# Twelve split halves, a Newton root on VectorE and modulation rows along the free axis, in a three-layer transformer kernel

## The chip, the cores and the metric

The kernel runs on one core of a Trainium2 chip as one program. The metric is device time in microseconds: the median of 3 runs of the kernel before is 1167.11 us (1166.7 to 1167.43). The engines are TensorE (PE, with weight loads shown apart as PEld), VectorE (DVE), ScalarE (ACT), GpSimd (POOL) and SyncE (SP), which here only issues DMAs.

## The reference, in short

256 tokens of width 1024 in f32 go through two layers of one kind and one of another.

```python
for l in range(2):
    h = rms_norm(x, g_pre_mix[l]);  z = h @ w_in[l]          # q, k, v, cb, cc, cx, ga, gb
    y_attn = band_attention(rope(q), rope(k), v, sink) @ w_attn_proj[l]
    y_conv = (cb * short_conv(cc * cx, conv_w[l])) @ w_conv_proj[l]
    mix = (sigmoid(ga) * y_attn + sigmoid(gb) * y_conv) @ w_out[l]
    x = x + rms_norm(mix, g_post_mix[l])
    h = rms_norm(x, g_pre_ffn[l])
    x = x + rms_norm((silu(h @ w_gate[l]) * (h @ w_up[l])) @ w_down[l], g_post_ffn[l])
mod = silu(c) @ w_cond + b_cond                              # 6 rows of 1024: shift, scale, gate, twice
h = rms_norm(x, g_mix_pre) * (1 + scale_m) + shift_m
mix = concat(stick_breaking(q, k, v), pooling(u)) @ w_out;   x = x + gate_m * rms_norm(mix, g_mix_post)
h = rms_norm(x, g_ffn_pre) * (1 + scale_f) + shift_f
x = x + gate_f * rms_norm((silu(h @ w_gate) * (h @ w_up)) @ w_down, g_ffn_post)
```

`rms_norm(x, g)` is `x * rsqrt(mean(x*x) + 1e-6) * g`, along the row of a token.

## The kernel before, in words

**Split products.** Every f32 product is made of two or three products of a rounded type. A value is cast to its high part H on ACT (`nc.scalar.copy`, L277 for weights, L208 for activations) and DVE subtracts to get the low part L (L279, L209). Then H x H, H x L and L x H are added up in PSUM.

**The weight stream.** The host packs all weights in the order of use into chunks of 128 x 2048 f32 (1 MB, `ORDER`). `emit_raw` (L250) issues one DMA for a chunk on SP's queue into one of `NRAW` = 4 buffers (the first four chunks in two halves each). `emit_half` (L266) splits half a chunk into an H and an L tile of 128 x 1024; there are `NSPLIT` = 9 of each. `get` (L283) hands out the next chunk, and emits loads up to 5 chunks and splits up to 3 chunks ahead; its `cap` bounds the splits, at L506 and L587 to `NSPLIT` halves counted from the oldest chunk still held. `behind` (L262) places a split in its engine's order after a named instruction: ACT's casts after the last square of the latest norm, DVE's subtractions after its scaling.

**Order.** The program hands its instructions to a framework, which fixes each engine's order at build time from the program's order, the dependencies and its own estimates; on the chip each engine keeps to that order. The program itself interleaves independent work by generators with due times on a clock of PE work (`spawn`, `tick`, `pe`): the transposes of a norm (`Norm.tr`) come `TR_DELAY` = 6.0 us of PE work after the post norm before them. `hp()` raises the priority of the norms' operations.

**Norms.** The tokens lie in two tiles of 128, t = 0 and 1, in `xt`. A stage's output products fill two PSUM halves for t = 0, then two for t = 1 (`row_out`, L486: 3 chunks x 2 halves x 6 products for each tile). After each half, `Post.half` squares and sums it on ACT (`sumsq`, L354, and a small add, L355) and multiplies it by the gain row on DVE (L422). `Post.fin` takes the root (`rstd`, L358: a power of -0.5 on POOL, L360) and adds the scaled half to x on DVE (L429). Then `Norm.vec` does the same for the next norm: squares on ACT, x times the gain row on DVE (L378), the root on POOL, the scaling on DVE (L384; L386 with a shift row; L382 for the very first norm, whose gain is applied after the transposes, L401). PE transposes the result (L395), ACT and DVE split it (`Pair.put`, L208 and L209), and the next stage's products can begin. In the FFN these are `pgA` and `puA` for t = 0 (24 products each), then for t = 1.

**Start.** 13 products on ones run first, then the first norm, then `q_first` (L700), the q projection in an order of its own.

**Conditioning.** The six modulation rows are computed beside layers 0 and 1. `cond_chunk` (L516) takes 256 rows of `w_cond` at a time, adds w times silu(c), a column scalar, into an accumulator of 128 x 1024 (L527, twice a chunk, 24 chunks), then GpSimd sums it over the partitions (L530), and a row goes to DRAM (`modd`). `get_rows` (L965) fetches the gain and modulation rows for the next norm by DMA, broadcast over the partitions, where the last three down chunks' outputs begin; it is called from `mkpost`.

**Buffers.** Large activation tiles (4 KB a partition) come from a pool of `NS4` = 17.

Of the kernel before, what the change touches and what calls it, by code (L numbers as in the profile page):

```python
# [10 lines left out]
F32 = mybir.dt.float32  # L11
F32R = mybir.dt.float32r
AF = mybir.ActivationFunctionType
ALU = mybir.AluOpType
# [20 lines left out]
WARM = 13  # L35
NRAW = 4
NSPLIT = 9
LOOK = 3
LOOK_RAW = 5
NS4 = 17  # L40
NS2 = 7
# [75 lines left out]
def pack_weights(inp):  # L117
# [10 lines left out]
    for i, k in enumerate(ORDER):  # L128
# [31 lines left out]
def tile_model(ctx: ExitStack, tc: tile.TileContext, x_in, wpack, sink, convw, gains, c_in, g0t_in,  # L160
# [101 lines left out]
    def behind(e):  # L262

        return tc.issue_after(state["behind"][e].ins) if state["behind"] and state["spl"] + e else nullcontext()

    def emit_half():  # L266
        i, hf = divmod(state["spl"], 2)
        while state["raw"] <= i:
            emit_raw()
        if ORDER[i][0] == "cond":  # L270
            HL[i] = raws[i]
        else:
            H = wp.tile([P, CH // 2], F32R, tag="H", name=f"H{i}_{hf}", bufs=NSPLIT)
            L = wp.tile([P, CH // 2], F32R, tag="L", name=f"L{i}_{hf}", bufs=NSPLIT)
            rv = raws[i][:, hf * (CH // 2):(hf + 1) * (CH // 2)]
            with behind(0):
                nc.scalar.copy(H, rv)  # L277
            with behind(1):
                nc.vector.tensor_sub(L, rv, H.bitcast(F32))  # L279
            HL.setdefault(i, []).append((H, L))  # L280
        state["spl"] += 1

    def get(key, cap=None):  # L283
# [3 lines left out]
        n = len(ORDER)  # L287
        while state["raw"] < min(i + LOOK_RAW, n):
            emit_raw()
# [16 lines left out]

    warm = cst.tile([P, 512], mybir.dt.bfloat16, tag="warm", name="warm")
    nc.vector.memset(warm, 1.0)
# [7 lines left out]
    for i in range(WARM):  # L316
        mm(pw, warm[:, 0:P], warm, i == 0, i == WARM - 1)
    emit_raw()
    emit_raw()
    nc.sync.dma_start(xt[1], x_in[P:2 * P, :])  # L320
    nhalf = cst.tile([P, 1], F32, tag="nhalf", name="nhalf")
    nc.vector.memset(nhalf, -0.5)
    eps = cst.tile([P, 1], F32, tag="eps", name="eps")
# [3 lines left out]
    modd = dr.tile([6, D], F32, tag="modd", name="modd")  # L327
    silu_c = cst.tile([P, KT], F32, tag="silu_c", name="silu_c")
# [4 lines left out]
    csb = cst.tile([P, KT], F32, tag="csb", name="csb")  # L333
    pscale = cst.tile([P, 4], F32, tag="pscale", name="pscale")

    def late_consts():
# [5 lines left out]
        nc.sync.dma_start(cw, convw)  # L342
        nc.sync.dma_start(csb, c_in)
        nc.sync.dma_start(pscale, pool_scale)
# [6 lines left out]
    def sumsq(src, c, ssq, name):  # L351

        junk = s2(f"jk_{name}{c}")
        nc.scalar.activation(junk, src, AF.Square, scale=D ** -0.5, accum_out=ssq[:, c:c + 1])  # L354
        return nc.scalar.activation(ssq[:, c:c + 1], ssq[:, c:c + 1], AF.Identity,  # L355
                                    bias=eps if c == 0 else ssq[:, 0:1])

    def rstd(ssq, name):  # L358
        rs = small("rs_" + name, 1)
        nc.gpsimd.tensor_tensor(rs, ssq[:, 1:2], nhalf, ALU.pow)  # L360
        return rs

    class Norm:
# [6 lines left out]
        def vec(self):  # L370
            t, name = self.t, self.name
            with hp():
                ssq = small("sx_" + name, 2)
                xg = s4("xg_" + name)
                for c in range(2):
                    self.sq = sumsq(xt[t][:, HC[c]], c, ssq, "x" + name)
                    if self.cols is None:
                        nc.vector.tensor_mul(xg[:, HC[c]], xt[t][:, HC[c]], self.G[:, HC[c]])  # L378
                rs = rstd(ssq, "x" + name)
                for c in range(2):  # L380
                    if self.cols is not None:
                        self.sc = nc.vector.tensor_scalar(xg[:, HC[c]], xt[t][:, HC[c]], rs[:, 0:1], None, ALU.mult)  # L382
                    elif self.S is None:
                        self.sc = nc.vector.tensor_scalar(xg[:, HC[c]], xg[:, HC[c]], rs[:, 0:1], None, ALU.mult)  # L384
                    else:
# [123 lines left out]

    cacc = [None]  # L510

    def cond_due():
# [3 lines left out]
    def cond_chunk(key):  # L516
        w = get(key).rearrange("p (h k c) -> p k h c", k=2, h=2)
        r, j = key[1], key[2]
        if j == 0:
            a = s4(f"cacc{r}")  # L520
            nc.vector.memset(a, 0.0)
            nc.scalar.dma_start(a[0:1, :], b_cond[r:r + 1, :])
            cacc[0] = a
        a = cacc[0]
        for k in range(2):
            a3 = a.rearrange("p (h c) -> p h c", h=2)
            nc.vector.scalar_tensor_tensor(a3, w[:, k], silu_c[:, 2 * j + k:2 * j + k + 1], a3, ALU.mult, ALU.add)  # L527
        if j == 3:
            mrow = s4(f"mrow{r}")
            nc.gpsimd.partition_all_reduce(mrow, a, P, bass_isa.ReduceOp.add)  # L530
            nc.scalar.dma_start(modd[r:r + 1, :], mrow[0:1, :])

    def ffn(l, xp, norms, make_post, after):
        order = [k for k in ORDER if k[0] in ("g", "u", "d") and k[1] == l]
# [27 lines left out]
        for key in order:  # L562
# [137 lines left out]
    def q_first(q, xp):  # L700
# [28 lines left out]
        spawn(norms[1].gen, 1.0)  # L729
        w[1, 0] = get(("q", 0, 1, 0), 8)  # L730
        run(0, 1, (0,))
# [9 lines left out]
    def mixer1(l, xp, norms):  # L741
# [198 lines left out]


    xp = Pair("x0")
    norms = [Norm(t, None, None, xp, f"n0{t}", g0t) for t in range(2)]
# [3 lines left out]
    for l in range(DEPTH):  # L947
# [43 lines left out]

        ffn(l, xp, norms, mkpost, after2)
        xp, norms = nxp, nn
# [121 lines left out]
```

## Time and profile before

| | |
|---|---|
| median of 3 runs | 1167.11 us (1166.7 to 1167.43) |
| profiled execution: own time, span | 1168.2 us, 1166.2 us |
| mean granted clock of TensorE | 0.996 |
| PE busy | 1147.2 us, 98% |
| DVE, ACT, POOL busy | 829.4, 694.7, 55.3 us |
| read from HBM | 232.76 MB, 201 GB/s over the span |

In rows of instructions, the first two numbers are the start in the span and the duration, in us; "x4" is a count of merged instructions; what stands in brackets at the end is how long the engine was idle before, and what ended that. In rows of waits, the numbers are the total, the count and the longest, in us. In rows of stretches, each engine has its busy time and count, and then come PE's granted clock, the busy share of the DMA engines and GB/s. A matmul's end is modelled, so neighbouring matmuls overlap: from one start to the next counts, not the duration.

### The profile page before, as it was taken

The page shows a single profiled execution, that of the slowest core. Times are in us where ns is not written, and L with a number is a line of the kernel's source. Part 1 is how long each engine was busy: PE and PEld are TensorE (multiplying, and loading weights), DVE is VectorE, ACT ScalarE, POOL GpSimd, SP SyncE. Part 2 cuts the span into 40 slices and gives each one's busy share as a digit, 9 for nine tenths or more (in the row PEclk, how much of TensorE's full clock was granted, in tenths as well). Part 3 has the DMA queues.
Part 4 walks back from the last instruction along what each step waited for, and adds up shares of the span by engine and source line. Part 5 has one row for each costly group of instructions (what it writes and reads, how often), then busy time and mean ns, then how long its engine had stood idle before and what let it go on. Part 6 is the DMA issues. An engine that isn't in the chain of part 4 may idle for free.

```text
span 1166.2 us, 15511 instructions
## 1 busy us (share of the span) xinstructions
PE 1147.2 (98%) x5909; PEld 957.3 (82%) x5909; DVE 829.4 (71%) x1149; ACT 694.7 (60%) x1219; POOL 55.3 (5%) x34
## 2 busy tenths in 40 slices
PE   8999999999999999999999999999999999999997
PEld 5888888878888887888888878888877777888886
DVE  6788835869788858787757678887958438766652
ACT  6777856556555447688856456545456546655451
POOL 0000000001102000000020002020200001000000
PEclk8999999999999999999999999999999999999999
DMA  9633335657576664534457647675766245654620
GB/s 330 257 144 113 141 144 210 228 212 266 204 290 221 249 250 181 217 114 139 145 190 290 226 146 268 246 271 212 286 230 248 104 162 181 253 184 177 211 79 36
DMA packets 36386, 234.83 MB, mean 201 GB/s; under 512 B 4812, under 2 KB 5324, under 8 KB 9816
## 3 DMA queue, kind: packets, MB, share of 16 engines
q1 hardware_dynamic: 33552, 224.82, 52.9%
q10 hardware_dynamic: 2760, 9.03, 2.4%
q8 instruction: 46, 0.75, 0.3%
q14 instruction: 28, 0.23, 0.1%
HBM read 232.76 MB, written 1.07 MB: 201 GB/s over the span
## 4 chain that ended last, share of the span: by engine, by line
PE 89%; ACT 4%; DVE 3%; DMA 1%; issue 1%; POOL 1%; SPq 0%; DVEq 0%; POOLq 0%; ACTq 0%
PE pu L244 14%; PE dn L244 14%; PE pg L244 13%; PE pq L244 4%; PE pcx L244 4%; PE pcp L244 4%; PE wo L244 4%; PE pap L244 4%; PE pga L244 4%; PE pgb L244 4%; PE pcb L244 3%; PE pgA L244 2%; PE puA L244 2%; PE pcc L244 2%; PE pkv L244 2%; PE po L244 2%
## 5 line engine op out<-in xcount | busy, mean ns | idle before, releaser
L279 DVE TENSOR_TENSOR L<-raw,H 128x1024 fp32r<-128x1024 f32 x374 | 470.8, 1271 | 182.5 <-ACT H L277 171.3
L277 ACT CAST H<-raw 128x1024 fp32r<-128x1024 f32 x374 | 390.0, 1050 | 182.9 <-PE pg L244 35.5
L244 PE MATMUL dn<-H,fHL 128*128 128x512 f32 x432 | 116.1, 390 | 0.0
L244 PE MATMUL pu<-xf,H 128*128 128x512 f32 x432 | 108.2, 392 | 0.0
L244 PE MATMUL pg<-xf,H 128*128 128x512 f32 x432 | 107.8, 391 | 0.0
L244 PEld LDWEIGHTS dn<-H,fHL 128*128 128x128 f32 x432 | 79.8, 188 | 15.6
L244 PEld LDWEIGHTS pg<-xf,H 128*128 128x128 f32 x432 | 79.2, 188 | 15.2
L244 PEld LDWEIGHTS pu<-xf,H 128*128 128x128 f32 x432 | 77.7, 189 | 13.9
L244 PE MATMUL dn<-L,fHL 128*128 128x512 f32 x216 | 66.6, 389 | 0.0
L244 PEld LDWEIGHTS pg<-xf,L 128*128 128x128 f32 x432 | 58.9, 190 | 4.2
L244 PEld LDWEIGHTS pu<-xf,L 128*128 128x128 f32 x432 | 58.9, 190 | 4.2
L527 DVE SCALAR_TENSOR_TENSOR cacc<-raw,silu_c,cacc 128x1024 f32<-128x1024 f32 x48 | 61.3, 1277 | 0.2
L244 PE MATMUL pu<-xf,L 128*128 128x256 f32 x432 | 60.2, 282 | 0.0
L244 PE MATMUL pg<-xf,L 128*128 128x256 f32 x432 | 60.2, 282 | 0.0
L530 POOL PARTITION_ALL_REDUCE mrow<-cacc x6 | 38.9, 6489 | 346.6 <-PE po L244 138.3
L244 PE MATMUL wo<-H,m 128*128 128x512 f32 x192 | 52.4, 395 | 0.0
L573 ACT CAST fHL<-f 128x512 fp32r<-128x512 f32 x27 | 16.7, 619 | 56.1 <-DVE f L571 56.1
L244 PEld LDWEIGHTS dn<-L,fHL 128*128 128x128 f32 x216 | 40.6, 188 | 8.6
L244 PEld LDWEIGHTS wo<-H,m 128*128 128x128 f32 x192 | 35.5, 188 | 7.4 <-DVE m L209 0.2
L567 ACT ACTIVATE s<-s 128x512 f32<-128x512 f32 x27 | 17.1, 632 | 33.0 <-DVE s L454 33.0
L244 PE MATMUL pcp<-H,y 128*128 128x512 f32 x128 | 35.4, 396 | 0.0
L244 PE MATMUL pap<-H,o 128*128 128x512 f32 x128 | 35.2, 394 | 0.0
(283 smaller groups left out, 1980.4 us busy)
## 6 DMA issues: line engine op xcount, KB each, us to landing
raw<-in_wpack_dram SPq DMA_DIRECT2D x207, 1024.0 KB, 5.0
raw<-in_wpack_dram SPq DMA_DIRECT2D x8, 512.0 KB, 7.0
gpm<-in_gains_dram ACTq DMA_DIRECT2D x3, 512.0 KB, 6.2
gpf<-in_gains_dram ACTq DMA_DIRECT2D x3, 512.0 KB, 9.2
gqf<-in_gains_dram ACTq DMA_DIRECT2D x2, 512.0 KB
out_dram<-x SPq DMA_DIRECT2D x4, 256.0 KB, 2.0
pmat<-in_pmat_dram SPq DMA_DIRECT2D x2, 384.0 KB, 5.9
x<-in_x_dram SPq DMA_DIRECT2D x2, 256.0 KB, 2.9
```

The source lines that it names most:

```text
L244: nc.tensor.matmul(o, a, b, start=start, stop=stop, **kw)
L277: nc.scalar.copy(H, rv)
L279: nc.vector.tensor_sub(L, rv, H.bitcast(F32))
L527: nc.vector.scalar_tensor_tensor(a3, w[:, k], silu_c[:, 2 * j + k:2 * j + k + 1], a3, ALU.mult, ALU.add)
L530: nc.gpsimd.partition_all_reduce(mrow, a, P, bass_isa.ReduceOp.add)
L567: last = nc.scalar.activation(s, s, AF.Silu)
L573: nc.scalar.copy(fHL[:, 0], fv)
```

## The change

- Raw weights come in halves of a chunk: 8 buffers of 128 x 1024, one DMA each. There are 12 H and 12 L tiles instead of 9. The large activation tiles fall from 17 to 15; the build reserves less scratch, and some constants move into pools.
- The very first split cast is placed behind the first norm's squares on ACT.
- `sumsq` keeps one small add (mean + eps of the first half) and drops the second; `rstd` now adds, guesses the root by integer operations and takes three Newton steps, nine operations on DVE, in place of the power on POOL. In norms without a shift row the gain is multiplied in the scaling itself (scalar_tensor_tensor) and not before it.
- Conditioning weights are packed so that a partition holds output columns and the input runs along the free axis. silu(c) is a row broadcast to all partitions (in a large activation tile), DVE multiplies and sums along the row in one operation per half chunk, and the reduction on GpSimd goes. c and b_cond are now fetched on ACT's queue in layer 0's gates.
- `get_rows` is also called at the down chunk five before the end (`early`), two chunks before the tail.

```diff
-NRAW = 4
-NSPLIT = 9
+NRAW = 8
+NSPLIT = 12
-NS4 = 17
+NS4 = 15
...
         elif n == "cond":
-            put(i, inp["w_cond_2"][0], 256 * k[2], 2, 1024 * k[1], 1024)
+            w = inp["w_cond_2"][0][:, 1024 * k[1]:1024 * (k[1] + 1)].reshape(D, P, KT)
+            out[i].reshape(P, 2, D)[...] = w[:, :, 2 * k[2]:2 * k[2] + 2].transpose(1, 2, 0)
...
     def emit_raw():
-        i = state["raw"]
-        t = wp.tile([P, CH], F32, tag="raw", name=f"raw{i}", bufs=NRAW)
-        n = 2 if i < 4 else 1
-        for h in range(n):
-            hs = slice(h * CH // n, (h + 1) * CH // n)
-            if i == 0 and h == 1:
-                nc.vector.tensor_copy(t[:, hs.start:hs.start + 1], xt[0][:, 0:1])
-            state["dma"] = nc.sync.dma_start(t[:, hs], wpack[i][:, hs])
-        raws[i] = t
+        i, hf = divmod(state["raw"], 2)
+        t = wp.tile([P, CH // 2], F32, tag="raw", name=f"raw{i}_{hf}", bufs=NRAW)
+        if state["raw"] == 1:
+            nc.vector.tensor_copy(t[:, 0:1], xt[0][:, 0:1])
+        state["dma"] = nc.sync.dma_start(t, wpack[i][:, hf * (CH // 2):(hf + 1) * (CH // 2)])
+        raws[2 * i + hf] = t
         state["raw"] += 1
 
     def behind(e):
-        return tc.issue_after(state["behind"][e].ins) if state["behind"] and state["spl"] + e else nullcontext()
+        if state["spl"] + e == 0:
+            return tc.issue_after(norms[0].sq.ins)
+        return tc.issue_after(state["behind"][e].ins) if state["behind"] else nullcontext()
...
     def sumsq(src, c, ssq, name):
         junk = s2(f"jk_{name}{c}")
-        nc.scalar.activation(junk, src, AF.Square, scale=D ** -0.5, accum_out=ssq[:, c:c + 1])
-        return nc.scalar.activation(ssq[:, c:c + 1], ssq[:, c:c + 1], AF.Identity,
-                                    bias=eps if c == 0 else ssq[:, 0:1])
+        i = nc.scalar.activation(junk, src, AF.Square, scale=D ** -0.5, accum_out=ssq[:, c:c + 1])
+        if c == 0:
+            i = nc.scalar.activation(ssq[:, 0:1], ssq[:, 0:1], AF.Identity, bias=eps)
+        return i
 
     def rstd(ssq, name):
-        rs = small("rs_" + name, 1)
-        nc.gpsimd.tensor_tensor(rs, ssq[:, 1:2], nhalf, ALU.pow)
-        return rs
+        w = small("nw_" + name, 3)
+        m, y, t = (w[:, i:i + 1] for i in range(3))
+        nc.vector.tensor_scalar(m, ssq[:, 1:2], ssq[:, 0:1], -0.5, ALU.add, ALU.mult)
+        nc.vector.tensor_scalar(y.bitcast(I32), m.bitcast(I32), 0x7FFFFFFF, 1, ALU.bitwise_and, ALU.logical_shift_right)
+        nc.vector.tensor_scalar(y.bitcast(I32), y.bitcast(I32), -1, 0x5F3759DF - (1 << 22), ALU.mult, ALU.add)
+        for _ in range(3):
+            nc.vector.scalar_tensor_tensor(t, y, m, y, ALU.mult, ALU.mult)
+            nc.vector.scalar_tensor_tensor(y, t, 1.5, y, ALU.add, ALU.mult)
+        return y
...
-                    if self.cols is None:
+                    if self.S is not None:
                         nc.vector.tensor_mul(xg[:, HC[c]], xt[t][:, HC[c]], self.G[:, HC[c]])
...
                     elif self.S is None:
-                        self.sc = nc.vector.tensor_scalar(xg[:, HC[c]], xg[:, HC[c]], rs[:, 0:1], None, ALU.mult)
+                        self.sc = nc.vector.scalar_tensor_tensor(xg[:, HC[c]], xt[t][:, HC[c]], rs[:, 0:1],
+                                                                 self.G[:, HC[c]], ALU.mult, ALU.mult)
...
     def cond_chunk(key):
-        w = get(key).rearrange("p (h k c) -> p k h c", k=2, h=2)
+        w = get(key)
         r, j = key[1], key[2]
-        if j == 0:
-            a = s4(f"cacc{r}")
-            nc.vector.memset(a, 0.0)
-            nc.scalar.dma_start(a[0:1, :], b_cond[r:r + 1, :])
-            cacc[0] = a
-        a = cacc[0]
-        for k in range(2):
-            a3 = a.rearrange("p (h c) -> p h c", h=2)
-            nc.vector.scalar_tensor_tensor(a3, w[:, k], silu_c[:, 2 * j + k:2 * j + k + 1], a3, ALU.mult, ALU.add)
+        for u in range(2):
+            nc.vector.scalar_tensor_tensor(w[u], w[u], 1.0, silu_c, ALU.mult, ALU.mult,
+                                           accum_out=mcol[:, r, 2 * j + u:2 * j + u + 1])
         if j == 3:
-            mrow = s4(f"mrow{r}")
-            nc.gpsimd.partition_all_reduce(mrow, a, P, bass_isa.ReduceOp.add)
-            nc.scalar.dma_start(modd[r:r + 1, :], mrow[0:1, :])
+            nc.vector.tensor_add(mcol[:, r], mcol[:, r], bcol[:, r])
+            nc.scalar.dma_start(modd[r].rearrange("(p j) -> p j", p=P), mcol[:, r])
 
-    def ffn(l, xp, norms, make_post, after):
+    def ffn(l, xp, norms, make_post, after, early=lambda: None):
...
+                if j == NDOWN - TAIL - 2:
+                    early()
...
-        w[1, 0] = get(("q", 0, 1, 0), 8)
+        w[1, 0] = get(("q", 0, 1, 0), 6)
...
             if l == 0 and c == 0:
+                csb = s4("csb")
+                nc.scalar.dma_start(csb, c_in[0].partition_broadcast(P))
+                nc.scalar.dma_start(bcol, b_cond)
                 nc.scalar.activation(silu_c, csb, AF.Sigmoid)
                 nc.vector.tensor_mul(silu_c, silu_c, csb)
...
+    silu_c = s4("silu_c")
...
-        ffn(l, xp, norms, mkpost, after2)
+        ffn(l, xp, norms, mkpost, after2, get_rows)
...
-    nc = _bacc.Bacc("TRN2", target_bir_lowering=False, num_devices=1)
+    nc = _bacc.Bacc("TRN2", target_bir_lowering=False, num_devices=1, dynamic_dma_scratch_size=1024)
```

More of the change, by code (lines that the diff above doesn't have):

```diff
@@ L12 @@
 F32R = mybir.dt.float32r
+I32 = mybir.dt.int32
 AF = mybir.ActivationFunctionType
@@ L250, in emit_raw @@
     def emit_raw():
[L251 to L259 removed]
+        i, hf = divmod(state["raw"], 2)
[4 more added lines that the diff above has]
+        raws[2 * i + hf] = t
         state["raw"] += 1
     def behind(e):
[L264 removed]
+        if state["spl"] + e == 0:
+            return tc.issue_after(norms[0].sq.ins)
+        return tc.issue_after(state["behind"][e].ins) if state["behind"] else nullcontext()
     def emit_half():
[L267 to L268 removed]
+        n = state["spl"]
+        i, hf = divmod(n, 2)
+        while state["raw"] <= n:
             emit_raw()
+        r = raws.pop(n)
         if ORDER[i][0] == "cond":
[L271 removed]
+            HL.setdefault(i, []).append(r)
         else:
@@ L287, in get @@
         n = len(ORDER)
-        while state["raw"] < min(i + LOOK_RAW, n):
+        while state["raw"] < 2 * min(i + LOOK_RAW, n):
             emit_raw()
@@ L305, in row @@
         return g
-    warm = cst.tile([P, 512], mybir.dt.bfloat16, tag="warm", name="warm")
+    warm = s2("warm", (P, 512), mybir.dt.bfloat16)
     nc.vector.memset(warm, 1.0)
@@ L317, in tile_model @@
         mm(pw, warm[:, 0:P], warm, i == 0, i == WARM - 1)
-    emit_raw()
-    emit_raw()
+    for i in range(4):
+        emit_raw()
     nc.sync.dma_start(xt[1], x_in[P:2 * P, :])
-    nhalf = cst.tile([P, 1], F32, tag="nhalf", name="nhalf")
-    nc.vector.memset(nhalf, -0.5)
     eps = cst.tile([P, 1], F32, tag="eps", name="eps")
@@ L327, in tile_model @@
     modd = dr.tile([6, D], F32, tag="modd", name="modd")
-    silu_c = cst.tile([P, KT], F32, tag="silu_c", name="silu_c")
+    mcol = cst.tile([P, 6, KT], F32, tag="mcol", name="mcol")
+    bcol = cst.tile([P, 6, KT], F32, tag="bcol", name="bcol")
     amask = cst.tile([P, 2, P], F32, tag="amask", name="amask")
@@ L332, in tile_model @@
     cw = cst.tile([P, DEPTH, KT, 3], F32, tag="cw", name="cw")
-    csb = cst.tile([P, KT], F32, tag="csb", name="csb")
     pscale = cst.tile([P, 4], F32, tag="pscale", name="pscale")
@@ L508, in mix_out @@
         row_out(ch, accs, lead > 0, make_post, after)
-    cacc = [None]
     def cond_due():
@@ L1095 @@
         ("gains", np.stack(g)),
-        ("c", inp["c_2"].reshape(KT, P).T),
+        ("c", inp["c_2"].reshape(1, D)),
         ("g0t", inp["g_pre_mix"][0].reshape(KT, P).T),
-        ("b_cond", inp["b_cond_2"].reshape(6, D)),
+        ("b_cond", inp["b_cond_2"].reshape(6, P, KT).transpose(1, 0, 2)),
         ("w_pool", inp["w_pool_2"][0].transpose(1, 0, 2)),
```

6 lines of the change are left out of this document (2 added, 4 removed).

## The prediction

> **What bounds the kernel now.** I read the page's busy shares first, then TensorE's own waits.
>
> ```profile
> span 1166.2 us, 15511 instructions
> PE 1147.2 (98%) x5909; PEld 957.3 (82%) x5909; DVE 829.4 (71%) x1149; ACT 694.7 (60%) x1219; POOL 55.3 (5%) x34
> ```
>
> ```profile
> PE pt_n L395 <- DVE xg_n L382: 2.3, 1, 2.3
> PE pt_nm L395 <- DVE xg_nm L386: 2.0, 2, 1.8
> PE pgA L244 <- DVE xf L209: 2.0, 3, 1.0
> ...
> PE pq L244 <- DVE xm L209: 0.9, 1, 0.9
> ```
>
> TensorE (PE) is busy for all but 1166.2 - 1147.2 = 19.0 us, and the change takes no product away, so everything it can win lies in those 19 us and in the time in which PE runs slowly. The waits lie at the norms: the first one (pt_n), the handovers where a norm feeds the next stage (pgA, pq), and the norm that needs modulation rows (pt_nm). The start in order of time, and then three stretches of it (busy times of PE, PEld, DVE, ACT, POOL, then PE's granted clock):
>
> ```profile
> 5.00 0.28 ACT L355 ACTIVATE sx_n<-sx_n,eps 128x1 f32<-128x1 f32 x1
> ...
> 6.74 1.04 ACT L277 CAST H<-raw 128x1024 fp32r<-128x1024 f32 x1 [1.46 <-DMA raw<-in_wpack_dram]
> ...
> 8.06 0.57 POOL L360 TENSOR_TENSOR rs_xn<-sx_n,nhalf 128x1 f32<-128x1 f32 x1 [7.63 <-ACT sx_n L355]
> 8.66 0.88 DVE L382 TENSOR_SCALAR xg_n<-x,rs_xn 128x512 f32<-128x512 f32 x2 [4.51 <-POOL rs_xn L360]
> ...
> 9.21 1.38 PE L395 MATMUL pt_n<-ident,xg_n 128*128 128x128 f32 x8 [2.33 <-DVE xg_n L382]
> ...
> 11.08 6.68 PE L244 MATMUL pq<-H,x 128*128 128x512 f32 x16 [0.49 <-ACT x L208]
> ```
>
> ```profile
> 6.88:9.20 2.32, 0.00 (x0) 0.00 (x0) 0.54 (x2) 1.10 (x2) 0.57 (x1) 1.00 0.85 279
> 9.87:16.69 6.82, 6.33 (x17) 4.30 (x16) 6.75 (x10) 5.66 (x9) 0.00 (x0) 0.50 1.04 389
> 16.69:25.30 8.61, 8.61 (x43) 7.12 (x42) 7.54 (x11) 5.68 (x13) 0.57 (x1) 1.00 0.97 371
> ```
>
> The sums of squares are ready by 5.28 but for one small add on ScalarE (ACT), and that add stands behind a split cast that waits for its weights until 6.74. Then PE stands still for 2.32 us, its clock is halved for 6.82 us, and DVE is nearly full (6.75 of 6.82, then 7.54 of 8.61).
>
> **The change part by part. Newton's price.** The new root is nine DVE operations on one column, each on the one before. No such chain is in the trace; the nearest rows are two dependent operations on four columns:
>
> ```profile
> 71.72 0.15 DVE L666 TENSOR_TENSOR den<-den,es 128x4 f32<-128x4 f32 x1
> 71.91 0.18 DVE L668 RECIPROCAL rd<-den 128x4 f32<-128x4 f32 x1
> ```
>
> From one start to the next 0.19 us; nine make 1.7. Bounds: 9 x 0.15, the bare duration, = 1.35, and 9 x 0.22, the reciprocal's 0.18 with the gap of 0.04 ahead of it, = 2.0. I take 1.7, the integer steps included. A quiet chain of the first token tile, from the post norm's last sum to the transposes:
>
> ```profile
> 248.22 0.60 ACT L354 ACTIVATE jk_apm<-wo 128x512 f32<-128x512 f32 x1 [3.06 <-PE wo L244]
> ...
> 248.71 0.20 ACT L354 ACTIVATION_READ_ACCUMULATOR jk_apm<-wo 128x1 f32 x1
> ...
> 248.94 0.69 DVE L422 TENSOR_TENSOR ag_pm<-wo,gpm 128x512 f32<-128x512 f32 x1 [3.39 <-ACT jk_apm L354]
> ...
> 249.90 1.41 DVE L429 SCALAR_TENSOR_TENSOR x<-ag_pm,rs_apm,x 128x512 f32<-128x512 f32 x2 [0.27 <-POOL rs_apm L360]
> ...
> 251.88 0.19 ACT L354 ACTIVATION_READ_ACCUMULATOR jk_xnf<-x 128x1 f32 x1
> ...
> 251.98 0.28 ACT L355 ACTIVATE sx_nf<-sx_nf,eps 128x1 f32<-128x1 f32 x1
> ...
> 253.25 0.88 DVE L384 TENSOR_SCALAR xg_nf<-xg_nf,rs_xnf 128x512 f32<-128x512 f32 x2 [0.73 <-POOL rs_xnf L360]
> ...
> 254.82 0.60 PE L395 MATMUL pt_nf<-ident,xg_nf 128*128 128x128 f32 x4
> ```
>
> Now ACT's add and GpSimd's power take from 248.91 to 249.90, 0.99 us, while DVE multiplies by the gain in their shadow. After, the multiplication (to 249.63) stands ahead of the root on the same engine: 0.72 + 1.7 = 2.4, so x starts at 251.35, 1.45 later. In the norm the second add on ACT goes: from the last sum (252.07) it is 1.18 to the scaling now; after, the one add left (to 252.26, 0.2) and 1.7, so 0.7 more. The scaling takes the gain in with it, two halves in 1.41 instead of 0.88, the first 0.3 later; the gain's own multiplication, which goes, lay beside ACT's squares. In all 2.4 us: the first half is ready at 253.7 now and near 256.2 then, against 254.82, when PE asks for it.
>
> **Handovers.** The first row is of the chain of waits, the others are of the timeline, where a subtraction that PE needs stood behind two splits:
>
> ```profile
> 237.27 16.37 PE wo L244 x72
> ```
>
> ```profile
> 255.78 2.35 DVE L279 TENSOR_TENSOR L<-raw,H 128x1024 fp32r<-128x1024 f32 x2
> ...
> 257.01 0.48 PE L244 MATMUL pgA<-H,xf 128*128 128x512 f32 x1
> ...
> 258.05 0.41 DVE L209 TENSOR_TENSOR xf<-pt_nf,xf 128x256 fp32r<-128x256 f32 x1
> ...
> 258.52 0.96 PE L244 MATMUL pgA<-H,xf 128*128 128x512 f32 x3 [0.80 <-DVE xf L209]
> ```
>
> Twelve halves let six of the next stage be split before the output products instead of three (caps at L506 and L587), so fewer stand there. What hides the longer chain is the second tile's output: 3 chunks x 2 halves x 6 products = 36, at 16.37/72 = 0.227 us, 8.2 us from about 248.1, just ahead of the square at 248.22, to 256.3. If the transposes are placed behind these products, PE has work until the data come at 256.2; transposes, cast and subtraction then put the next products near 257.6 without a split in front, near 258.8 with one (1.2), against 258.3 now (258.52 less the one product that slipped in at 257.01). From -0.7 to +0.5; I take -0.2 for each of the three (both mixes and the first FFN): **-0.6**. Bounds: -2.9, both wait rows gone, and 3 x 1.4 = +4.2, the transposes left where they are. The second tile's chain lies under the first tile's 48 gate and up products, 10.9 us; it grows by the same 2.4, which fits.
>
> **Start: -1.3.** With the cast behind the squares, Newton runs from 5.3 to 7.0, and the scaling starts 1.65 earlier than at 8.66. But the second norm's root now costs DVE 1.7 us in a stretch where it has only 8.61 - 7.54 = 1.1 us free, so some of it is given back. Bounds: 0, and -3.4 with the clock kept (below). **Modulation rows.**
>
> ```profile
> 860.85 0.36 ACTq L974 DMA_DIRECT2D scl_m<-modd  x1
> ...
> 867.09 1.23 DVE L975 SCALAR_TENSOR_TENSOR g2pre<-scl_m,g2pre 128x1024 f32<-128x1024 f32 x1 [4.83 <-DMA scl_m<-modd]
> ...
> 873.49 0.63 PE L395 MATMUL pt_nm<-ident,xg_nm 128*128 128x128 f32 x4 [1.80 <-DVE xg_nm L386]
> ```
>
> The row was issued so late that DVE waited 4.83 us and PE 1.80. It is now fetched two chunks earlier, each 24 products or 5.4 us, more than the wait. PE's wait of 2.0 in two goes, less what the longer chain takes: **-1.7**, bounds -2.0 and 0. **The power beside the splits.**
>
> ```profile
> 982.12 2.44 POOL L360 TENSOR_TENSOR rs_xnf<-sx_nf,nhalf 128x1 f32<-128x1 f32 x1 [2.89 <-ACT sx_nf L355]
> ...
> 985.40 0.66 PE L395 MATMUL pt_nf<-ident,xg_nf 128*128 128x128 f32 x4 [0.59 <-DVE xg_nf L386]
> ```
>
> Once the power took 2.44 us, and PE lost 0.59. Newton ends that, but its own longer chain comes back: **-0.4**, bounds -0.6 and +1.4. **Tail: +1.4.** At the end nothing covers the root:
>
> ```profile
> 1160.90 0.69 DVE L422 TENSOR_TENSOR ag_pf<-dn,gpf 128x512 f32<-128x512 f32 x1 [3.39 <-ACT jk_apf L354]
> ...
> 1161.92 1.41 DVE L429 SCALAR_TENSOR_TENSOR x<-ag_pf,rs_apf,x 128x512 f32<-128x512 f32 x2 [0.33 <-POOL rs_apf L360]
> ```
>
> 1160.90 + 0.69 + 1.7 = 1163.3 in place of 1161.92. Bounds +1.0 and +1.7, by the root's.
>
> **At nothing.** The conditioning sums, now 48 multiplications with a sum along the row, have the same shape as the old step in the page's groups; below it the stretch where they are thickest, and the page's row of the weight loads:
>
> ```profile
> L527 DVE SCALAR_TENSOR_TENSOR cacc<-raw,silu_c,cacc 128x1024 f32<-128x1024 f32 x48 | 61.3, 1277 | 0.2
> ```
>
> ```profile
> 200.00:230.00 30.00, 30.00 (x137) 24.68 (x136) 21.98 (x25) 15.46 (x19) 0.00 (x0) 1.00 0.74 271
> ```
>
> ```profile
> raw<-in_wpack_dram SPq DMA_DIRECT2D x207, 1024.0 KB, 5.0
> ```
>
> They hide under PE: DVE is busy 21.98 of 30 us there. The reduction over partitions on GpSimd goes, and nobody waited for it. Weight loads double in number, issued by SP, which has nothing else to do; a half's buffer comes free earlier. The fetch of c grows to a whole broadcast row, with b_cond beside it, both on ACT's queue. The large buffers fall from 17 to 15, one held by silu_c. Without cover, the price is that of a late row (rival D).
>
> [...]
>
> **Sum:** -1.3 - 0.6 - 1.7 - 0.4 + 1.4 = -2.6. The profiled execution took 1168.2 us by its own time, 2.0 outside its span, so 1165.6; it lies 1.1 over the median of the runs, 1167.11, so the forecast is **1164.5**.
>
> **Rivals.** *B, even:* DVE swallows the start's gain and the handovers gain nothing: -1.7 - 0.4 + 1.4 = -0.7, 1166.4. For it: DVE's 6.75 of 6.82 us. Against: 2.32 us of standstill that need no DVE. *C, slower, the chain outgrows its cover:* the first tile's transposes stay in their place in PE's order, 6.0 us of products after the post norm (TR_DELAY), and PE waits at each from 254.82 to 256.2: 1.4 at four handovers, 5.6 for -0.6 and the modulation row's gain down to -1.2: -1.3 + 5.6 - 1.2 - 0.4 + 1.4 = +4.1, **1171.2**. It decides from 1.1 us of lengthening (254.82 - 253.7); I count 2.4. Against it: 2.2 us of independent products could be put ahead. A split of 1.2 us between two links of the chain makes it worse. *D, a late row:* the fetch of c, a broadcast like scl_m (6.2 us to its use), holds ACT's queue, or a buffer is short: up to -2.6 + 6.2 = +3.6, 1170.7. *E, the clock is kept:* PE's standstill shrinks from 2.32 to about 0.7 us; if the half clock does not come, its 6.82 us give back up to 3.4, of which casts and DVE leave perhaps 2.0: -4.6, 1162.5.
>
> [...]
>
> **How the numbers follow.** The forecast 0.42, B 0.12, C 0.22, D 0.07, E 0.17. The forecast's own range is 1162.5 to 1166.8. A measurement of this kernel can tell 0.2%, 2.3 us, from no change, so faster means under 1164.8: 0.26 of the forecast and E, 0.43; same is the rest of it, B and 0.02 of C, 0.30; slower the rest of C and D, 0.27. The range, 1160.5 to 1172, reaches from below E to above C.
>
> **What would show it.** Right: the first transposes near 7.5; roots of 1.7 us on DVE; no wait for a modulation row; the end 1.4 us further behind the last product. Wrong: waits for xg in all handovers (C), the first cast still ahead of the root, ACT waiting for csb (D), or links of the root far apart with splits between them.

## The result: 55 us slower

The changed kernel takes 1221.93 us (median of 4 runs, 1220.55 to 1225.26) beside 1167.04 us of the kernel before on the same chip: a ratio of 1.0474, 95% interval 1.0453 to 1.0496. The forecast was 1164.5, in a range of 1160.5 to 1172.

The page of the changed kernel, the lines that answer to those shown of before:

```profile
span 1223.4 us, 16128 instructions
PE 1164.5 (95%) x5909; PEld 967.4 (79%) x5909; DVE 838.9 (69%) x1400; ACT 685.3 (56%) x1193; POOL 0.2 (0%) x4
```

PE's idle time rose from 19.0 to 58.9 us (+39.9), and its busy time, with the same 5909 products, by 17.3 us: it ran slower for a part of them (mean granted clock 0.979 for 0.996). TensorE's own waits in the changed kernel (total, count, longest, in us):

```profile
PE pt_nf L403 <- DVE xg_nf L391: 13.5, 4, 6.3
PE pgA L246 <- DVE xf L211: 7.5, 5, 2.1
PE PTp L680 <- ACT P L672: 7.4, 5, 5.2
PE pt_nm L403 <- DVE xg_nm L394: 5.7, 2, 4.8
PE pt_nm L403 <- DVE xg_nm L391: 4.4, 2, 3.8
PE pt_nf L403 <- DVE xg_nf L394: 4.1, 2, 3.8
PE pt_n L403 <- DVE xg_n L389: 1.8, 1, 1.8
```

Most of it is the norm's output xg, which comes too late for its transposes: 29.5 us of waits for 4.9 before, so 24.6 of the 39.9, and there mostly the second token tile's. The longest of these waits, 3.8 to 6.3 us, are all at t = 1. Behind them stand the waits for xf, the split of the transposed result out of PSUM (called its eviction below). One row is of another kind: PTp, the transposes of the softmax in attention. DVE's timeline of the changed kernel at the first handover (mixer 0 to FFN 0) shows the second tile's two roots:

```profile
259.27 0.20 DVE L362 TENSOR_SCALAR nw_apm<-sa_pm 128x1 f32<-128x1 f32 x1
...
260.72 0.14 DVE L364 TENSOR_SCALAR nw_apm<-nw_apm 128x1 int32<-128x1 int32 x1
260.78 1.21 DVE L281 TENSOR_TENSOR L<-raw,H 128x1024 fp32r<-128x1024 f32 x1
261.91 0.21 DVE L366 SCALAR_TENSOR_TENSOR nw_apm<-nw_apm 128x1 f32<-128x1 f32 x1
...
262.64 1.22 DVE L281 TENSOR_TENSOR L<-raw,H 128x1024 fp32r<-128x1024 f32 x1
263.78 0.21 DVE L366 SCALAR_TENSOR_TENSOR nw_apm<-nw_apm 128x1 f32<-128x1 f32 x1
263.91 1.22 DVE L281 TENSOR_TENSOR L<-raw,H 128x1024 fp32r<-128x1024 f32 x1
265.04 0.15 DVE L367 SCALAR_TENSOR_TENSOR nw_apm<-nw_apm 128x1 f32<-128x1 f32 x1
...
267.52 0.15 DVE L367 SCALAR_TENSOR_TENSOR nw_apm<-nw_apm 128x1 f32<-128x1 f32 x1
267.59 1.21 DVE L281 TENSOR_TENSOR L<-raw,H 128x1024 fp32r<-128x1024 f32 x1
268.72 1.41 DVE L437 SCALAR_TENSOR_TENSOR x<-ag_pm,nw_apm,x 128x512 f32<-128x512 f32 x2
...
271.18 0.20 DVE L362 TENSOR_SCALAR nw_xnf<-sx_nf 128x1 f32<-128x1 f32 x1
271.31 1.21 DVE L527 SCALAR_TENSOR_TENSOR raw<-raw,silu_c 128x1024 f32<-128x1024 f32 x1
...
275.65 1.41 DVE L391 SCALAR_TENSOR_TENSOR xg_nf<-x,nw_xnf,gpf 128x512 f32<-128x512 f32 x2
278.94 1.22 DVE L527 SCALAR_TENSOR_TENSOR raw<-raw,silu_c 128x1024 f32<-128x1024 f32 x1 [1.87 <-DMA raw<-in_wpack_dram]
```

In five of the eight gaps between the links of the post norm's root the build has placed a split of 1.2 us, and in the others short evictions or a product with the gain row. This root, nine links that took 1.98 us where nothing stood between them (the first tile's, from 253.90 to 255.88), lasts from 259.27 to 267.67, 8.4 us; the next norm's, with two conditioning products and an eviction between its links, from 271.18 to 275.61. Before, the second tile's x was added at 260.78; now at 268.72. The last row is a second thing: a conditioning product stands in DVE's order in front of the evictions of xf and waits 1.87 us for weights that have not landed.

Where the 57.2 us of the two spans lie, stage by stage: each number is the later start of a stage's first product than before, less what the stages ahead of it had lost already. The edges are the first products of the gates (`pgb`, layers 0 and 1), of the FFNs' `pg`, of layer 1's `pkv` and of mixer 2's `wo`, and the last product. Columns: the changed kernel, and six of the experiments below.

| us | changed | e1 | e4 | e6 | e7 | e8 | e3 |
|---|---|---|---|---|---|---|---|
| start and layer 0's attention | +0.1 | -1.3 | -1.4 | -1.1 | -1.3 | -2.8 | -0.4 |
| mixer 0 to FFN 0 | +12.6 | +0.3 | +0.6 | +2.9 | +10.2 | +1.6 | +8.0 |
| FFN 0 to mixer 1 | +6.5 | +0.4 | +0.2 | +1.2 | +5.1 | +0.9 | +3.7 |
| layer 1's attention | +9.4 | +8.1 | +0.8 | +9.9 | +8.1 | +8.0 | +9.7 |
| mixer 1 to FFN 1 | +12.0 | +0.2 | +0.1 | +2.5 | +10.3 | +1.5 | +9.1 |
| FFN 1 to mixer 2, and mixer 2 | +5.9 | -2.0 | -2.5 | 0.0 | +2.6 | -0.7 | +2.8 |
| mixer 2 to FFN 2 | +9.2 | +2.6 | +1.9 | +3.8 | +6.5 | +2.2 | +7.4 |
| last down products | -0.2 | -0.2 | -0.2 | -0.2 | -0.2 | +0.8 | -0.2 |
| tail | +1.7 | +0.4 | +0.4 | +0.3 | +1.9 | +1.8 | +1.8 |

The five handovers make 46.2 us (12.6 + 6.5 + 12.0 + 5.9 + 9.2), layer 1's attention 9.4 and the tail 1.7.

### The profile page after: what moved, and what is told of

It reads as the page before. It is cut to its first block, busy times and chain, and to the rows that moved or that the text cites. A ratio compares the mean times of both kernels' runs of the same rounds, so it can differ in the third digit from the quotient of the medians.

```text
span 1223.4 us, 16128 instructions
## 1 busy us (share of the span) xinstructions
PE 1164.5 (95%) x5909; PEld 967.4 (79%) x5909; DVE 838.9 (69%) x1400; ACT 685.3 (56%) x1193; POOL 0.2 (0%) x4
## 4 chain that ended last, share of the span: by engine, by line
PE 82%; DVE 9%; ACT 4%; DMA 3%; issue 2%; SPq 0%; DVEq 0%; ACTq 0%
PE dn L246 13%; PE pu L246 13%; PE pg L246 12%; PE pcp L246 4%; PE pap L246 4%; PE pga L246 4%; PE pgb L246 4%; PE pcx L246 3%; PE pcb L246 3%; PE wo L246 3%; DVE L L281 3%; PE pcc L246 2%; PE pq L246 2%; DMA raw<-in_wpack_dram 2%; PE pgA L246 2%
## 5 line engine op out<-in xcount | busy, mean ns | idle before, releaser
L281 DVE TENSOR_TENSOR L<-raw,H 128x1024 fp32r<-128x1024 f32 x374 | 454.2, 1222 | 176.4 <-ACT H L279 161.2
L527 DVE SCALAR_TENSOR_TENSOR raw<-raw,silu_c 128x1024 f32<-128x1024 f32 x48 | 58.4, 1220 | 28.6 <-DMA raw<-in_wpack_dram 28.6
L246 PEld LDWEIGHTS pu<-xf,L 128*128 128x128 f32 x432 | 58.9, 190 | 4.2
L246 PEld LDWEIGHTS pg<-xf,L 128*128 128x128 f32 x432 | 58.9, 190 | 4.2
L246 PE MATMUL pgA<-H,xf 128*128 128x512 f32 x96 | 33.0, 463 | 7.5 <-DVE xf L211 7.5
```

The source lines that it names most:

```text
L246: nc.tensor.matmul(o, a, b, start=start, stop=stop, **kw)
L281: nc.vector.tensor_sub(L, r, H.bitcast(F32))
L527: nc.vector.scalar_tensor_tensor(w[u], w[u], 1.0, silu_c, ALU.mult, ALU.mult, accum_out=mcol[:, r, 2 * j + u:2 * j + u + 1])
```

## The experiments

Two theories stood at first. N: the second tile's root, cut open by other work on DVE, costs the handovers. R: conditioning products that wait in DVE's order for late weights cost them, and the attention.

**e1: POOL's root back, all else changed.**

```diff
-        w = small("nw_" + name, 3)
...
-        return y
+        rs = small("rs_" + name, 1)
+        nc.gpsimd.tensor_tensor(rs, ssq[:, 1:2], nhalf, ALU.pow)
+        return rs
```

> The changed kernel with one part undone: the root is a power on POOL again (with the second small add on ACT), everything else stays changed. Theory N (the cut chain): on DVE the nine links of the second tile's roots are cut open by other work (in the changed kernel 9 rows between the first and the last link of the second tile's post norm, 5 of them split subtractions of 1.22 us), and the 46 us that the five handovers lost, with the half clock behind them, come from that; without the links they come back: 1164 to 1168. Theory R (late conditioning weights): DVE stands in its order at the conditioning products for weights that have not landed (28.6 us in 23 waits, 0.2 before), with evictions that PE needs behind them; that stays, with the 9.4 us that layer 1's attention lost and the evictions' waits: 1176 to 1185.

1178.03 us, 1.0084 (1.0069 to 1.0099) of before. The time lies in R's range, but each theory holds by half: the handovers come back to within 0.4 us in three of five (table, e1), as N says, while the 8.1 us in layer 1's attention stay, as R says. PE's longest wait of e1:

```profile
PE PTp L675 <- ACT P L667: 7.4, 5, 5.2
```

DVE's timeline of e1 there, and under it ACT's:

```profile
555.31 0.15 DVE L654 SCALAR_TENSOR_TENSOR nm<-m,negsink 128x4 f32<-128x4 f32 x1
...
566.70 0.41 DVE L632 TENSOR_TENSOR qs<-q,qs 128x256 fp32r<-128x256 f32 x1
```

```profile
567.15 0.47 ACT L660 ACTIVATE P<-S,nm 128x256 f32<-128x256 f32 x1 [1.46 <-DVE qs L632]
```

The exponentials have their input at 555.46, but ACT starts them at 567.15, released by qs, which they do not read. qs is the last reader of q, a large tile; P is a large tile too. So a third theory, S: the exponentials wait for q's tile, since of 15 large tiles one is held by silu(c). e4 and e11 test it.

**e2: Newton alone in the kernel before** (the nine operations and one small add on ACT less; nothing else).

> The kernel before with one part of the change alone: the Newton root on DVE (and one small add on ACT less). Theory N: the second tile's chains are cut open here too (10, 10, 10, 11 and 6 rows between the links of the five post norms in the order of the build), so most of the loss comes with this part alone: 1205 to 1218, PE's waits for xg at 20 us or more. Theory R: only the longer chain shows, as rival C of the prediction had it: 1169 to 1174.

1202.97 us, 1.030 (1.0284 to 1.0315): 35 of the 55 us come with the root alone, a little less than N expected. e1 lost 10 without Newton, so 10 more belong to both together.

**e6 and e7: Newton for one tile only, in the changed kernel.**

```diff
+        if name[-1] == "1":          # e7: "0"
+            rs = small("rs_" + name, 1)
+            nc.gpsimd.tensor_tensor(rs, ssq[:, 1:2], nhalf, ALU.pow)
+            return rs
```

> The changed kernel with Newton's root for the first token tile only; the second tile's roots are on POOL. Theory N (cut chains in the second tile): all that is left of the handovers' loss is the first tile's longer chain, a wait of 0.4 to 0.9 us at each of five, beside what the first experiment left: 1178 to 1184. If DVE's added work counts, wherever it stands, about half of the 44 us between the changed kernel and the first experiment stays: 1195 to 1203.

> The mirror image: Newton's root for the second token tile only, the first tile's on POOL. Theory N: nearly the whole loss stays, 1212 to 1222, with PE's waits for xg before the second tile's transposes at 3 to 6 us each. If DVE's added work counts wherever it stands: 1195 to 1203.

e6 takes 1185.67 us (1.0155; 1.014 to 1.0171), 7.6 over e1, and e7 1211.01 (1.0377; 1.0363 to 1.0392), 33 over e1. Four fifths belong to the second tile, whose chain runs while DVE also does the first tile's evictions and the next stage's splits. The first tile's chain runs in a quieter stretch (in the changed kernel DVE is busy for 6.36 of the 9.5 us from 247.5 to 257.0); e6 loses 1.2 to 3.8 us at four handovers, and the modulation row's gain is gone at the fifth. e7 lies 1 us under N's range, e6 1.7 over its.

**e3: the splits held behind the second tile's scaling too.**

```diff
-            if t == 0:
+            if True:
                 state["behind"] = (norms[t].sq, norms[t].sc)
```

> The changed kernel, Newton root and all, with the splits emitted after the second tile's norm also placed behind that tile's scaling (the changed kernel places them behind the first tile's alone). In the order of the build no split is left between the links; 4, 4, 4, 5 and 1 short rows are. Theory N: the handovers come down to the longer chain itself, 1170 to 1185. Theory R: DVE's waits for conditioning weights stay where they are: 1205 or more. A third way: the splits that are held back come late for PE, and its waits move from xg to L: 1190 to 1225.

1209.43 us, 1.0349 (1.0332 to 1.0366): only 12.5 us better. DVE's timeline of e3, and after it one row of PE's:

```profile
257.67 0.21 DVE L362 TENSOR_SCALAR nw_apm<-sa_pm 128x1 f32<-128x1 f32 x1
...
260.87 1.42 DVE L437 SCALAR_TENSOR_TENSOR x<-ag_pm,nw_apm,x 128x512 f32<-128x512 f32 x2
...
265.23 1.41 DVE L391 SCALAR_TENSOR_TENSOR xg_nf<-x,nw_xnf,gpf 128x512 f32<-128x512 f32 x2
266.56 9.16 DVE L281 TENSOR_TENSOR L<-raw,H 128x1024 fp32r<-128x1024 f32 x8
275.65 0.74 DVE L211 TENSOR_TENSOR xf<-pt_nf,xf 128x256 fp32r<-128x256 f32 x2
```

```profile
276.12 1.43 PE L246 MATMUL pgA<-H,xf 128*128 128x512 f32 x3 [2.40 <-DVE xf L211]
```

The chain is now whole: x at 260.87, where the kernel before had 260.78, and the transposes wait 0.6 us instead of 6.3. But eight splits, five of which had stood between the links of the post norm's root, now stand in one block of 9.16 us ahead of the evictions, and PE waits for those, and for H and L of the weights. By the time alone R would fit too (1205 or more); by PE's waits it was the third way of the expectation, and N in its first form falls: it isn't the places of the splits alone, it is the work. One stretch of the kernel before, and the same stretch of the changed kernel (busy times of PE, PEld, DVE, ACT, POOL, then the granted clock):

```profile
259.00:277.00 18.00, 18.00 (x87) 14.87 (x86) 16.67 (x25) 12.11 (x23) 1.10 (x2) 1.00 0.63 232
```

```profile
259.00:277.00 18.00, 11.26 (x49) 9.10 (x50) 17.67 (x40) 8.43 (x15) 0.00 (x0) 0.95 0.76 260
```

Before, DVE has 1.33 us free in 18; afterwards 0.33. Two roots of 2 us each don't fit there without pushing other work out of the stretch. Theory C from here on: DVE is full there, and Newton's time is added to what PE waits for.

**e8 and e9: the same without the splits' subtractions**, in the changed kernel and in the one before. The low part of every weight is left out (zeros stand in its place), PE's products stay.

```diff
-            L = wp.tile([P, CH // 2], F32R, tag="L", name=f"L{i}_{hf}", bufs=NSPLIT)
+            L = zl                   # one tile of zeros
...
-            with behind(1):
-                nc.vector.tensor_sub(L, r, H.bitcast(F32))
```

> The changed kernel without DVE's split subtractions: the low part of every weight is left out (one tile of zeros stands in for all of them), so DVE has 374 operations of 1.22 us less; PE's products are as many as before. Only for the question whether DVE's load beside the chain is what costs. Theory C (DVE is full at the handovers, so Newton's time there is added to what PE waits for): without the splits the chains run undisturbed and the evictions stand behind nothing: the handovers' 44 us go but for the longer chain, 1167 to 1180, according to what is left of the attention's 8.4. Theory L (the chain's own length costs, whatever else DVE has to do): 1195 or more.

> The kernel before with the same thing left out, as the measure for the run above: PE is busy for all but 19 us there, so both theories expect little, 1160 to 1166.

e8 takes 1180.92 us (1.0115; 1.01 to 1.013), 41 less than the changed kernel; e9 1165.45 (0.9982; 0.9972 to 0.9991). The same stretch in e8:

```profile
259.00:277.00 18.00, 17.87 (x84) 14.50 (x83) 12.26 (x35) 14.16 (x23) 0.00 (x0) 1.00 0.83 298
```

With DVE at 12.26 of 18 us four handovers cost 0.9 to 2.2 us each, Newton and all, and the fifth keeps 0.7 of the modulation row's gain; what stays is the attention's 8.0 and the tail. Theory L (1195 or more) falls. The time goes with theory C, 0.9 us over the upper end of its range, with the attention's loss in it. e8 takes away the load and with it the rows between the links; e3, which took away only the latter and moved the load behind them, gained 12.5. An order that keeps all the work and puts the evictions ahead of the held splits was not tried, so load and order are not wholly parted.

**e4 and e11: the large tiles.** Both have POOL's root and 11 split halves; e4 has 17 large tiles, e11 has 15.

```diff
-NSPLIT = 12
+NSPLIT = 11
-NS4 = 15
+NS4 = 17        # e4 only
```

> The kernel of the first experiment (changed, but with the power on POOL) with 17 large activation tiles again, as before, and 11 split halves instead of 12 to make room. With POOL's root 8.4 us stayed lost in layer 1's attention, where PE waited 5.2 us for the softmax on ACT, and ACT's row was released by qs on DVE. Theory S (tiles short): 15 tiles, one held by silu(c), leave 14 for the rest, and the softmax output waits for the tile that q held; with 17 it starts at once: 1168 to 1171. Theory R (late conditioning weights): the conditioning products stand in DVE's order beside that softmax whatever the tiles are: 1175 to 1180.

> The kernel of the fourth run with 15 large tiles instead of 17 and nothing else different (POOL's root, 11 split halves): the tiles by themselves. Theory S: the 8 us in layer 1's attention are back, 1176 to 1180. If the one split half fewer had mended it: 1168 to 1170.

e4: 1168.98 us, 1.0017 (1.0008 to 1.0026); e11: 1175.30, 1.0071 (1.0056 to 1.0086). The tiles alone make 6.3 us, and layer 1's attention holds all of it (+0.8 and +8.1); e11 lies 0.7 under S's range. PE's wait in e4, and ACT's start of the exponentials there:

```profile
PE PTp L675 <- ACT P L667: 2.3, 4, 1.6
```

```profile
555.63 0.48 ACT L660 ACTIVATE P<-S,nm 128x256 f32<-128x256 f32 x1
```

They start 0.13 us after their input (555.35 + 0.15 = 555.50), at once, where e1 had them 11.7 us late. S holds; that the tile they waited for is q's is read from what released them. R falls for the attention: the conditioning products are the same in both. It falls for the handovers too, as long as POOL has the root: in e4 DVE still waits 24.0 us in all ahead of the conditioning products, and four of its five handovers lose 0.6 us at most. e4 also bounds the rest of the change, raw weights and splits by halves and the new conditioning: with the start's and the rows' gains (1.4 and 2.5 us in the table) it stands 0.17% over the kernel before, so these parts cost 3.8 us by the table's rows and about 6 by the medians, 1.9 of them at mixer 2 to FFN 2.

**e5: two placements alone in the kernel before**, the first cast behind the squares and the early rows.

```diff
+        if state["spl"] + e == 0:
+            return tc.issue_after(norms[0].sq.ins)
...
+                if j == NDOWN - TAIL - 2:
+                    early()
```

> The kernel before with two small parts of the change alone: the first split cast behind the first norm's squares on ACT, and the rows for the next norm fetched at the down chunk five before the end. No Newton, no halves, nothing of the buffers. By the first experiment these gave 1.1 us at the start and 1.5 us at layer 2's first norm; if the parts add up: 1164 to 1165.5, PE's waits for xg_n and for xg_nm under 0.7 us together. If the early rows only hold tiles that others need, or the start's gain is given back by the casts: 1166.5 to 1169.

1166.10 us over 11 runs, 0.9988 (0.9979 to 0.9997): between the two expectations, and the only version here with all of the work that beats the kernel before, by 0.12%. By the same working as in the table the start gives 1.0 us and the rows 0.9, and 0.5 is lost again at mixer 2 to FFN 2. Three stretches of e5's start:

```profile
0.00:10.00 10.00, 7.78 (x25) 3.32 (x25) 4.09 (x15) 5.92 (x13) 0.76 (x5) 1.00 0.78 254
10.00:20.00 10.00, 7.41 (x29) 4.87 (x28) 7.12 (x9) 7.15 (x13) 0.56 (x1) 1.00 1.02 384
20.00:30.00 10.00, 10.00 (x49) 8.29 (x48) 7.55 (x11) 7.68 (x12) 0.00 (x0) 1.00 0.90 327
```

Here the clock stays at 1.00, where it was 0.50 for 6.82 us before. It brings little: from 10 to 20 us PE is busy for 7.41 of 10 us, with the DMA engines busy all the time (1.02), at 384 GB/s. That it waits there for H casts of weights that are still arriving is read from the changed kernel, where the cast has the same place and PE waits 1.3 us for them in its first 30 us.

**e10, e12, e13: is the slow clock the wait's own follow-up?** e10 puts 18 products on ones ahead of the second tile's transposes. e12 puts 20 of them, in the FFNs, strictly between the first tile's last product and the transposes; e13 is its control, with one.

```diff
+            if t == 1:
+                pd = ps1(f"dummy{l}")
+                with tc.issue_after(lastmm[0].ins):
+                    for i in range(NWARM):       # e12: 20, e13: 1
+                        dm = nc.tensor.matmul(pd, warm[:, 0:P], warm, start=True, stop=True)
+                with tc.issue_after(dm.ins):
+                    finish(norms[t].gen)
...
-            spawn(norms[t].gen, TR_DELAY)
+            if t == 0:
+                spawn(norms[t].gen, TR_DELAY)
```

> The changed kernel with 18 products on ones (4.1 us at 0.227 us each), whose result nobody reads, placed on PE ahead of each second tile's transposes but the very first, that is in the gaps in which PE waits 3.8 to 6.3 us for xg. Theory K (the clock falls because PE stands still): the gaps that are left are under 2.5 us, the clock stays up, and most of the 17 us by which PE's busy time grew come back: 1203 to 1212. If the slow clock has another cause, or the products only push the chain later: 1219 to 1228.

> As the tenth run, which filled the gaps only in part (3.47 us were left in two of them), but with 20 products on ones (4.5 us) bound to their place: in the three FFNs they come directly behind the first tile's last product and ahead of the second tile's transposes, which are no longer placed by their due time. In the changed kernel these gaps are 6.3, 6.3 and 3.8 us. Theory K (the clock falls because PE stands still): at most 1.9 us stay idle, the clock is kept at these three handovers, and about half of what the half clock costs in all comes back, 1209 to 1216. If the slow clock has another cause: 1219 to 1228.

> The control for the run above: the same placing with one product on ones instead of 20, so that the gaps stay open. Either way as the changed kernel, 1217 to 1226, with the clock halved behind each gap.

e10: 1218.71 us (1.0434; 1.0411 to 1.0458); e12: 1220.00 (1.0437; 1.0418 to 1.0456); e13: 1223.52 (1.0471; 1.0452 to 1.0489). In e10 the build put most of the products where PE was busy anyway, three waits of 3.1 to 3.5 us stayed, and the time lies just under the range for another cause: inconclusive. e12 is 3.5 us under its control, less than K expected; by its number it lies in the range for another cause. The granted clock over the span rose in each of its four runs, 0.987 to 0.989 for 0.977 to 0.980. At the first gap it did what K says. Control and e12, from the windows of each:

```profile
270.00:280.00 10.00, 2.89 (x10) 2.38 (x11) 7.94 (x21) 3.03 (x6) 0.00 (x0) 0.70 0.74 275
280.00:290.00 10.00, 10.00 (x38) 8.06 (x38) 7.34 (x12) 6.50 (x8) 0.00 (x0) 0.78 0.68 215
```

```profile
270.00:280.00 10.00, 6.56 (x34) 3.52 (x33) 8.30 (x22) 4.12 (x9) 0.00 (x0) 1.00 0.72 276
280.00:290.00 10.00, 10.00 (x45) 8.26 (x45) 9.78 (x14) 8.23 (x10) 0.00 (x0) 1.00 0.79 252
```

The half clock is gone and 3.2 us of the handover with it (12.4 to 9.2). At the second FFN the clock fell all the same (0.50 for 6.82 us), and at the third an eviction came 4.2 us late. So at one place of three the slow clock goes when the standstill is filled; that it follows from the standstill at the others is the author's estimate and not shown.

## Why the prediction was wrong, point by point

**The step that failed** is the sentence on the second tile's chain: it "lies under the first tile's 48 gate and up products, 10.9 us; it grows by the same 2.4, which fits". It asked how long PE had other work, and not how long DVE had. In that stretch DVE had 1.33 of 18 us free, by the row of the kernel before that stands above. Two roots of 2 us each, less some 0.8 us that the gain's own multiplication no longer takes (1.29, and the scaling 1.41 for 0.88), either push eight splits and the evictions behind them (e3) or are cut open by splits (the changed kernel). For three handovers I had put down -0.6 in all and a bound of +4.2; those three measured +31.1 (12.6 + 6.5 + 12.0) and all five +46.2, the half clock included. With DVE relieved, the same chains cost 0.9 to 2.2 each at four handovers (e8), near the 1.4 each of rival C and not the -0.2 of the forecast.

**Rival C** had the sign and named the mechanism in passing, "a split of 1.2 us between two links of the chain makes it worse", and gave it no price. The trace of before held the pattern: two splits in one row ahead of an eviction (255.78) and DVE nearly full at the start. Nine links offer eight such gaps.

**The term at nothing that was not nothing** is the large tiles: "from 17 to 15, one held by silu_c. Without cover, the price is that of a late row (rival D)". Rival D had "a buffer is short" among its cases, at 6.2 us and a chance of 0.07. It came, at 8 us in the table (7.3 between e4 and e11), and not where a row is fetched but in layer 1's attention. The prediction did not ask which stage would wait for a tile.

**Newton's price** was 1.7 us, bounds 1.35 to 2.0. Measured in the quiet first tile of the changed kernel:

```profile
253.90 0.22 DVE L362 TENSOR_SCALAR nw_xnf<-sx_nf 128x1 f32<-128x1 f32 x1 [0.98 <-ACT sx_nf L355]
...
255.88 1.41 DVE L391 SCALAR_TENSOR_TENSOR xg_nf<-x,nw_xnf,gpf 128x512 f32<-128x512 f32 x2
```

1.98, at the upper bound: 0.25 and 0.20 for a pair of steps, not 0.19 each. The first tile's xg half is ready at 256.63 for a forecast of 256.2, and the transposes start at 256.68 after a wait of 0.44: the order did put them behind the second tile's products, as assumed. The gain of 0.2 did not come; e6, Newton on the first tile alone, has +1.2 to +3.8 at four handovers and 0.0 at the one with the modulation row.

**Start, -1.3:** right in size for either part alone: e1 and e5, with the cast's place and without Newton, have -1.3 and -1.0; e2, with Newton and without the cast's place, has -0.9 by the same working, since the small add that stood behind the cast is gone there. In the changed kernel, with both, nothing is left of it (+0.1), and why is not shown. Rival E's clock came (1.00 throughout), its 2 us more did not: PE is busy for 7.41 of the 10 us from 10 to 20 there, beside a DMA share of 1.02.

**Modulation rows, -1.7:** right where the roots don't cover it, -2.0 in e1 and -0.9 in e5; in the changed kernel the wait for the row is gone from PE's list, and the chain's 4.8 us stands in its place.

**The power beside the splits, -0.4:** wrong. POOL's stall of 2.44 us on this root was cheaper than a chain in DVE's order: +9.2 at mixer 2 to FFN 2.

**Tail, +1.4:** +1.7, the upper bound, as Newton's price.

**Conditioning at nothing:** the page of the changed kernel has

```profile
L527 DVE SCALAR_TENSOR_TENSOR raw<-raw,silu_c 128x1024 f32<-128x1024 f32 x48 | 58.4, 1220 | 28.6 <-DMA raw<-in_wpack_dram 28.6
```

1220 ns for 1277 before, so the duration was right. But the waits of these products for weights, 28.6 us for 0.2 before, were not foreseen. Where evictions stand behind them, as at 278.94, they can cost PE time; how much was not tried by itself. With POOL's root all of the rest of the change costs some 3.8 to 6 us (e4).

**What stays open:** how the 10 us that belong to Newton and the other parts together divide, why the second filled gap lost its clock, and whether an order with fewer splits at the handovers would carry Newton's root; none of it was tried.

## What to carry to other kernels

Before a chain of small dependent operations moves onto an engine, read that engine's busy time in the stretch where the chain runs, and not only how long the consumer is covered: here DVE had 1.33 of 18 us free, and the chain was paid for twice, by its own time (1.98 us) and by what was placed between its links (8.4 us with it). A slow operation on an idle engine, such as POOL's power of 0.55 to 2.44 us here, can be the cheaper place (1178.03 us with it in e1, 1221.93 without). Buffers that are taken away can be paid for far from the change: here layer 1's attention lost 8 us, while layer 0's lost none (-1.3 in e1, -1.4 in e4), and why the one and not the other is not shown.

## What the runs showed of the hardware

In half-microsecond windows of the changed kernel the granted clock is 0.50 from 275.5 to 285.5, from 589.5 to 596.0 and from 1036.5 to 1046.5 us. Windows laid over these three stretches show the work in them, at mean granted clocks of 0.54, 0.52 and 0.53:

```profile
274.46:284.70 10.24, 6.54 (x19) 5.16 (x20) 7.22 (x18) 2.44 (x5) 0.00 (x0) 0.54 0.68 229
...
589.60:596.40 6.80, 6.38 (x23) 3.78 (x25) 2.84 (x8) 6.35 (x19) 0.00 (x0) 0.52 0.46 146
1035.90:1046.10 10.20, 7.59 (x22) 5.91 (x23) 5.59 (x9) 3.39 (x6) 0.00 (x0) 0.53 0.26 98
```

Before, the one such stretch at work lasted 6.82 us. The waits of 6.33, 5.16 and 3.76 us at these three places thus go with the loss of 3.0 to 3.6 us more, an estimate from PE's busy time in each row times what its granted clock lacks (6.54 x 0.46 to 7.59 x 0.47). e12 has two standstills of nearly one length, at its second gap and at its first. The first row is the stretch at half clock behind the second gap, the others are the two standstills:

```profile
732.38:739.20 6.82, 6.10 (x19) 4.67 (x18) 5.20 (x10) 2.90 (x6) 0.00 (x0) 0.50 0.57 174
729.48:731.51 2.03, 0.03 (x1) 0.00 (x0) 1.85 (x9) 0.00 (x0) 0.00 (x0) 1.00 0.88 297
274.05:276.05 2.00, 0.00 (x1) 0.01 (x1) 1.79 (x8) 0.00 (x0) 0.00 (x0) 1.00 1.01 414
```

The standstill of 2.03 us was followed by 6.82 us at a granted clock of 0.50, the one of 2.00 us by none (1.00 from 270 to 290, as in e12's rows above). What makes the difference is not shown.
